# A GELU MLP on one core: the second product by 15 block products for 18

## The chip, the cores and the metric

One core of a Trainium2 chip. The time is device microseconds of the program on that core, as the median of the runs; a profiled execution gives the trace from which everything else is read. Engines: PE multiplies (PEld is its weight load), DVE is the vector engine, ACT the scalar engine, POOL and SP issue transfers (POOL also has a few small operations).

## The reference

```python
def setup_inputs():
    batch, m, k, h, n = 16, 512, 768, 3072, 768     # x, w1, b1, w2: float32, random

def reference(x, w1, b1, w2):
    y = np.matmul(x, w1) + b1
    y = 0.5 * y * (1.0 + erf(y / np.sqrt(2.0)))
    return np.matmul(y, w2).astype(np.float32)
```

The 8192 rows of x go through 768 -> 3072 -> 768. The kernel multiplies in bfloat16 and sums in float32.

## The kernel before

The 8192 rows are cut into pairs of row blocks: ten pairs of 2 x 384 rows and a last one of 2 x 256. For each pair the first product fills `g` (3072 hidden values of the pair's rows, as 24 chunks of 128 hidden values, bf16), and then the second product reads `g`. A tile is 128 rows; a pair has six tiles, the last pair four.

**First product.** Pair 0 is computed plainly (`plain`: six matmuls of 384 columns for each of the 24 hidden chunks and each half). From pair 1 on, a 2 x 2 scheme with seven products P1 to P7 is used (`product1`): three matmuls each, 21 for one step j, and one step gives two hidden chunks for both halves. The scheme needs sums of x (`sum_x`, k = 0 to 3, into `xft`; P7 reads the last of them) and seven forms of each w1 block. The forms are made once on chip (`make_w1`: one copy by ACT and five block sums on DVE, twelve times), staged in whatever tile is free, written to the DRAM tensor `w1f`, and read back from there by SP into a ring of seven slots in `w1t` (`load_slot`, asked for when a slot's last product P3 has been issued). DVE evacuates three products of a step (P7, P2, P6), ACT one (P1), and ACT does the four gelus. Pair 1 does its first three steps plainly, since their w1 blocks are still raw in `w1t`.

**Second product.** Each of the three sub-blocks of a pair takes one tile of the upper half and one of the lower half, with the hidden dimension cut in two and the output columns in two: a 2 x 2 scheme with seven products (M1 to M7), each of 12 matmuls 128 x 128 x 384 (`part2`). Five of the left operands are sums of parts of `g` (`gsum`, DVE, 1536 elements per partition, into `st`), two are parts of `g` itself. The seven forms of w2 lie in `w2t`; five of them are made from the four raw blocks by DVE (`make_w2`). Each product has one evacuation (`evacuate`): five on DVE, two on ACT. There are three PSUM pools of 3, 3 and 2 buffers.

**Order.** All work is put in program order by hand (`inorder`), so each engine works through its own list. The first two products of the next pair, P1 and P7, are issued before the current pair's last product (`ahead`), to cover the evacuations at the boundary; the sums of x for the next pair stand behind the last sub-block's M1, M5 and M2:

```python
            rest(2, "M1", forms(1) if later else xsums(0, 1))
            rest(2, "M5", forms(1) if later else xsums(2))
            rest(2, "M2", forms(1) if later else xsums(3))
            rest(2, "M7")
            if nxt is not None and p > 0:
                ahead(p + 1)
            rest(2, "M6")
```

In pair 0 the `make_w1` calls lie among the plain products (three) and among the second product (six); the last three stand at the start of pair 1, ahead of its plain products. Loads of x, w1 and w2, and the output stores of all pairs but the last, are issued from POOL; the w1f stores, the slot loads, the transposes of x and the last pair's outputs from SP.

Of the kernel before, what the change touches and what calls it, by code (L numbers as in the profile page):

```python
# [14 lines left out]

WF = {"M3": 0, "M4": 1, "M1": 2, "M5": 3, "M2": 4, "M6": 5, "M7": 6}
# [3 lines left out]
SF = {"M1": 0, "M5": 1, "M2": 2, "M7": 3, "M6": 4}  # L28
BANK = {"M1": "Z", "M3": "Y", "M2": "Y", "M6": "Y", "M4": "X", "M5": "X", "M7": "X"}
# [3 lines left out]
def kernel(  # L33
# [19 lines left out]
    HW = 384  # L53
    SLOT = 7 * KH * P
    RAW = 4 * KH * P
    RING = 7
    PLAIN = 3
    GRP = 3 * KC * P
    FIRST = -(-PLAIN * RAW // SLOT)
# [10 lines left out]
    w2r = w2.rearrange("(hh j p) n -> p j hh n", p=P, hh=2)  # L70
# [8 lines left out]
    evp = ctx.enter_context(tc.tile_pool(name="evp", bufs=2))  # L79
    x1p = ctx.enter_context(tc.tile_pool(name="x1p", bufs=1))  # L80
    xbp = ctx.enter_context(tc.tile_pool(name="xbp", bufs=2))
    dram = ctx.enter_context(tc.tile_pool(name="dram", bufs=1, space=bass.MemoryType.DRAM))
    ps_x = ctx.enter_context(tc.tile_pool(name="ps_x", bufs=3, space=bass.MemoryType.PSUM))
    ps_y = ctx.enter_context(tc.tile_pool(name="ps_y", bufs=3, space=bass.MemoryType.PSUM))
    ps_z = ctx.enter_context(tc.tile_pool(name="ps_z", bufs=2, space=bass.MemoryType.PSUM))

    w1f = dram.tile([HP, P, SLOT], BF16, name="w1f")
    w2t = keep.tile([P, HP, 7, NB], BF16, name="w2t")
    w1t = keep.tile([P, RING * SLOT], BF16, name="w1t")
    xt = keep.tile([P, KC, 2, HW], BF16, name="xt")  # L90
    xft = keep.tile([P, 5, KH, HW], BF16, name="xft")
    g = keep.tile([P, HC, 2, HW], BF16, name="g")
    st = keep.tile([P, 5, HP, P], BF16, name="st")
    tt = keep.tile([P, 2, 4, HW], FP32, name="tt")
    ot = keep.tile([P, 4, N], FP32, name="ot")
    b1t = keep.tile([P, HC], FP32, name="b1t")
    ident = keep.tile([P, P], BF16, name="ident")
# [15 lines left out]

    def bank(t, m):
        b = BANK[m]
        if b not in t:
            pool = {"X": ps_x, "Y": ps_y, "Z": ps_z}[b]
            t[b] = pool.tile([P, 512], FP32, name="ps" + b.lower())
        return t[b]

    def evacuate(t, m, n, c):
        ps = t[BANK[m]][:, :n]
        if m == "M4":
            t["x1"] = x1p.tile([P, HW], FP32, name="x1")
            copy("act", t["x1"][:, :n], ps)
        elif m == "M3":
            t["q"] = evp.tile([P, HW], FP32, name="q")
            add(t["q"][:, :n], t["x1"][:, :n], ps)
        elif m == "M1":
            t["z"] = evp.tile([P, HW], FP32, name="z")  # L130
            copy("act", t["z"][:, :n], ps)
        elif m == "M5":
            sub(c["12"], ps, t["q"][:, :n])
        elif m == "M2":
            sub(c["21"], ps, t["q"][:, :n])
        elif m == "M7":
            sub(c["11"], t["z"][:, :n], ps)
        else:
            sub(c["22"], t["z"][:, :n], ps)

# [9 lines left out]

    def moving1(m, kc, w):
        if m in XRAW:
            kh, half = XRAW[m]
            return xt[:, kh * KH + kc, half, :w]
        return xft[:, XF[m], kc, :w]

    def gelu1(j, h, half, src, w, sign):
        hc = h * HP + j  # L160
        inorder(nc.scalar.activation(out=g[:, hc, half, :w], in_=src, func=ACTF.Gelu,  # L161
                                     bias=b1t[:, hc:hc + 1], scale=sign))

    def product1(t, m, p, j, w):
        if m == "P1":
            t["c12"] = ps_z.tile([P, 512], FP32, name="psz")
            ps = t["c12"]
        elif m == "P4":
            ps = t["c12"]
        elif m == "P7":  # L170
            t["c22"] = ps_y.tile([P, 512], FP32, name="psy")
            ps = t["c22"]
        elif m == "P5":
            ps = t["c22"]
        else:
            ps = t["c11"]
# [6 lines left out]
        ps = ps[:, :w]  # L183
        if m == "P1":
            t["c11"] = ps_x.tile([P, 512], FP32, name="psx")
            copy("act", t["c11"][:, :w], ps)
        elif m == "P7":
            t["v"] = evp.tile([P, HW], FP32, name="z")
            copy("dve", t["v"][:, :w], ps)
        elif m == "P2":  # L190
            sub(t["c22"][:, :w], ps, t["v"][:, :w])
        elif m == "P6":
            sub(tt[:, j % 2, 0, :w], ps, t["v"][:, :w])
        elif m == "P4":
            gelu1(j, 1, 0, ps, w, 1.0)
        elif m == "P3":
            load_slot((p - 1) * HP + j - PLAIN + RING)
            gelu1(j, 0, 0, ps, w, 1.0)
        elif m == "P5":
            gelu1(j, 0, 1, tt[:, j % 2, 0, :w], w, -1.0)  # L200
            gelu1(j, 1, 1, ps, w, -1.0)


    def rows(h, half, i, j0=0, j1=HP):
        return g[:, h * HP + j0:h * HP + j1, half, i * P:(i + 1) * P]

    def gsum(m, i, j0=0, j1=HP):
        dst = st[:, SF[m], j0:j1, :]
        a11, a21 = rows(0, 0, i, j0, j1), rows(0, 1, i, j0, j1)
        a12, a22 = rows(1, 0, i, j0, j1), rows(1, 1, i, j0, j1)  # L210
        if m == "M1":
            add(dst, a11, a22)
        elif m == "M5":
            add(dst, a11, a12)
        elif m == "M2":
            add(dst, a21, a22)
        elif m == "M7":
            sub(dst, a22, a12)
        else:
            sub(dst, a11, a21)  # L220

    def part2(t, m, i, j0, j1):
        ps = bank(t, m)
# [381 lines left out]
```

## Time and profile before

| | |
|---|---|
| median of 3 runs | 903.23 us (902.63 to 903.81) |
| profiled execution | 901.76 us |
| its span, first to last instruction | 900.0 us |
| granted PE clock | 1.000 |
| PE busy | 890.6 us, 99% of the span |
| DVE busy | 479.8 us, 53% |
| ACT busy | 371.1 us, 41% |
| POOL busy | 81.4 us, 9% |
| second product's matmuls (L231) | 2688 |
| first product's matmuls (L179) | 2457 |

A group's line names the line of the kernel, the engine, the operation, the tiles (output <- inputs), the shapes and the count, then the busy time in total, the mean of one in ns, and the idle time of the engine just before these instructions with what ended it. Lines L101, L108 and L111 are the helpers `copy`, `add` and `sub`, so their groups are told apart by the tiles: `st<-g` is a sum for the second product, `ot<-...` an evacuation, `xft<-xt` a sum of x. A matmul's shown duration (326 ns) contains the pipeline behind it; matmuls follow each other closer than that. "DVE ot <- PE psx" at the end of a line means that the instruction started when PE's write to psx was done. POOL and SP show only the issue of a transfer; the page's last part has the median time to its landing.

### The profile page before, as it was taken

How to read it: one execution, taken by the hardware profiler on the slowest of the kernel's cores; microseconds unless marked ns; L12 is line 12 of the kernel's file. 1: busy time of each engine (PE TensorE's matmuls, PEld its weight loads, DVE VectorE, ACT ScalarE, POOL GpSimd, SP SyncE). 2: the span in 40 equal slices, each digit the busy share in tenths (PEclk: the TensorE clock that was granted, in tenths of full speed). 3: DMA queues.
4: the chain of work that ended last, by engine and by line, in shares of the span. 5: the costliest groups of instructions: out<-in, count | busy, mean ns of one | idle time of the engine just before them, and what ended most of it. 6: DMA issues, size and time to landing. Idle time of an engine off the chain costs nothing.

```text
span 900.0 us, 14009 instructions
## 1 busy us (share of the span) xinstructions
PE 890.6 (99%) x5627; PEld 544.6 (61%) x5627; DVE 479.8 (53%) x844; ACT 371.1 (41%) x726; POOL 81.4 (9%) x148
## 2 busy tenths in 40 slices
PE   7999999999999999999999999999999999999998
PEld 5656656666666666666666666665666666666774
DVE  1287744654555374456455544654564455446445
ACT  3542473057117503730671175047206702740550
POOL 5201100100110010001001100100100011000000
PEclk9999999999999999999999999999999999999999
DMA  9997976456817674673567267646636682673501
GB/s 163 207 232 180 391 268 173 109 161 202 179 62 211 203 134 112 201 174 101 174 212 158 74 208 193 141 118 211 157 94 194 204 147 86 215 176 104 163 27 71
DMA packets 89158, 148.30 MB, mean 165 GB/s; under 512 B 50796, under 2 KB 68228, under 8 KB 89092
## 3 DMA queue, kind: packets, MB, share of 16 engines
q1 hardware_dynamic: 65588, 101.77, 38.7%
q0 software_dynamic: 23504, 45.62, 22.9%
q8 instruction: 44, 0.72, 0.3%
q14 instruction: 22, 0.18, 0.1%
HBM read 124.56 MB, written 33.42 MB: 176 GB/s over the span
## 4 chain that ended last, share of the span: by engine, by line
PE 98%; DMA 1%; ACT 0%; POOL 0%; issue 0%; DVE 0%; ACTq 0%; POOLq 0%
PE psx L231 21%; PE psy L231 21%; PE psx L179 18%; PE psz L179 12%; PE psy L179 12%; PE psz L231 7%; PE psy L337 3%; PE psx L337 3%; DMA st<-in_x_dram 1%; PE psy L400 0%; ACT g L161 0%; PE psx L400 0%; PE psz L366 0%; DVE psy L111 0%; POOL st L76 0%
## 5 line engine op out<-in xcount | busy, mean ns | idle before, releaser
L179 PEld LDWEIGHTS <-w1t 128*128 128x128 bf16 x2457 | 240.2, 98 | 147.4 <-issue 0.8
L231 PEld LDWEIGHTS <-st 128*128 128x128 bf16 x1920 | 187.9, 98 | 124.0
L231 PE MATMUL psx<-w2t,st 128*128 128x384 bf16 x768 | 135.3, 326 | 0.0
L231 PE MATMUL psy<-w2t,st 128*128 128x384 bf16 x768 | 135.3, 326 | 0.0
L179 PE MATMUL psx<-xft,w1t 128*128 128x384 bf16 (+1 forms) x702 | 131.0, 320 | 0.0
L111 DVE TENSOR_TENSOR tt<-psx,z 128x384 f32<-128x384 f32 (+1 forms) x117 | 63.6, 544 | 103.0 <-PE psx L179 103.0
L101 ACT COPY x<-psx 128x384 f32<-128x384 f32 x32 | 15.3, 478 | 229.0 <-PE psx L231 228.0
L231 PEld LDWEIGHTS <-g 128*128 128x128 bf16 x768 | 75.1, 98 | 50.0 <-issue 0.6
L101 ACT COPY psx<-psz 128x384 f32<-128x384 f32 (+1 forms) x117 | 53.0, 453 | 94.4 <-PE psz L179 94.4
L108 DVE TENSOR_TENSOR st<-g 128x1536 bf16<-128x1536 bf16 (+2 forms) x116 | 91.7, 812 | 0.0
L111 DVE TENSOR_TENSOR psy<-psx,z 128x384 f32<-128x384 f32 (+1 forms) x117 | 64.7, 553 | 49.3 <-PE psx L179 47.6
L103 DVE COPY z<-psy 128x384 f32<-128x384 f32 (+1 forms) x117 | 63.7, 544 | 39.3 <-PE psy L179 39.2
L161 ACT ACTIVATE g<-psx,b1t 128x384 bf16<-128x384 f32 (+1 forms) x117 | 66.6, 569 | 38.5 <-PE psx L179 37.0
L161 ACT ACTIVATE g<-psz,b1t 128x384 bf16<-128x384 f32 (+1 forms) x117 | 66.5, 569 | 26.6 <-PE psz L179 26.6
L76 POOL DMA_DIRECT2D xb<-in_x_dram x58 | 31.2, 542 | 499.4 <-DMA xt<-xb 491.9
L161 ACT ACTIVATE g<-tt,b1t 128x384 bf16<-128x384 f32 (+1 forms) x117 | 70.9, 606 | 11.5 <-DVE tt L111 11.5
L179 PE MATMUL psx<-xt,w1t 128*128 128x384 bf16 (+1 forms) x351 | 74.2, 320 | 0.2
L179 PE MATMUL psz<-xt,w1t 128*128 128x384 bf16 (+1 forms) x351 | 74.2, 321 | 0.0
L179 PE MATMUL psy<-xt,w1t 128*128 128x384 bf16 (+1 forms) x351 | 74.2, 321 | 0.0
L179 PE MATMUL psy<-xft,w1t 128*128 128x384 bf16 (+1 forms) x351 | 74.2, 321 | 0.0
L179 PE MATMUL psz<-xft,w1t 128*128 128x384 bf16 (+1 forms) x351 | 74.2, 321 | 0.0
L231 PE MATMUL psx<-w2t,g 128*128 128x384 bf16 x384 | 74.2, 326 | 0.0
(58 smaller groups left out, 653.3 us busy)
## 6 DMA issues: line engine op xcount, KB each, us to landing
w1t<-w1f SPq DMA_DIRECT2D x117, 672.0 KB, 5.3
out_dram<-ot POOLq DMA_DIRECT2D x60, 384.0 KB, 2.6
xb<-in_x_dram POOLq DMA_DIRECT2D x58, 192.0 KB, 4.0
w2t<-in_w_dram POOLq DMA_DIRECT2D x8, 576.0 KB, 22.5
w1t<-in_w_dram POOLq DMA_DIRECT2D x7, 576.0 KB, 19.0
w1f<-tt SPq DMA_DIRECT2D x6, 672.0 KB, 5.6
w1f<-xft SPq DMA_DIRECT2D x4, 672.0 KB, 4.8
out_dram<-ot SPq DMA_DIRECT2D x4, 384.0 KB, 2.5
```

What stands on the lines that cost most here:

```text
L76: inorder(queue.dma_start(out=out, in_=in_))
L101: inorder(nc.scalar.copy(out=dst, in_=src))
L103: inorder(nc.vector.tensor_copy(out=dst, in_=src))
L108: inorder(nc.vector.tensor_tensor(out=dst, in0=a, in1=b, op=ALU.add))
L111: inorder(nc.vector.tensor_tensor(out=dst, in0=a, in1=b, op=ALU.subtract))
L161: inorder(nc.scalar.activation(out=g[:, hc, half, :w], in_=src, func=ACTF.Gelu, bias=b1t[:, hc:hc + 1], scale=sign))
L179: inorder(nc.tensor.matmul(out=ps[:, :w], lhsT=forms[:, W1F[m], kc, :], rhs=moving1(m, kc, w), start=(kc == 0 and m in ("P1", "P7")), stop ...
L231: inorder(nc.tensor.matmul(out=ps[:, :NB], lhsT=lhs, rhs=w2t[:, j, WF[m], :], start=(j == 0 and m in ("M1", "M3", "M4")), stop=(j == HP - ...
L337: inorder(nc.tensor.matmul(out=py[:, :HW], lhsT=lhs[:, kc, (j % 3) * P:(j % 3 + 1) * P], rhs=xt[:, kc, half, :], start=(kc == 0), stop=(kc ...
```

## The change

The second product goes from a 2 x 2 scheme to one with blocks of 3 x 3 x 2: a group is three row tiles; the hidden dimension is cut into three pieces of 8 chunks, the output columns into two halves. Plain blocks would take 18 block products; the scheme takes 15 (M0 to M14), each of 8 matmuls 128 x 128 x 384.

- A pair has two groups, G0 (the upper half's tiles) and G1 (the lower half's). The last pair has one group and one tile that is left over and computed plainly, but for two differences of its parts that go with raw w2 blocks.
- Six left operands are parts of `g` as they are (M14, M8, M4, M7, M6, M13). Nine are sums, made by 15 DVE instructions of 1024 elements; three of the nine (M3, M11, M0) are made in place in `g`, six in `st` (seven slots of 1024). `place_h` orders the hidden chunks in `g` so that each piece is contiguous.
- Of the 15 forms of w2 in `w2t`, four are raw blocks and eleven are made by DVE.
- Products share PSUM buffers in chains: A holds M4, then M12, M10 and M11 on top of it; B holds M13, M1, M9, M0; C M14, M2; D M8, M3; M5, M6 and M7 have one each. After each link the buffer's running sum is added to its place in the output tile. Per group: 6 copies on ACT, 12 additions on DVE.
- All PSUM buffers come from one pool of eight.
- The sums EARLY (M2a, M3a) and MIDDLE (M12, M2b, M10a, M11a, M11b) of a pair are spread over the later steps of its first product (`fill`, behind P2 and P6).
- The sums of x for the next pair now stand behind the second group's M3, M10, M9 and M11; `ahead` follows, then M0.
- To make room, the ring of w1 slots has five places for seven, and raw w1 groups 2 and 3 lie in `xft`. `make_w1` is staged in other tiles: three calls after the plain group 3, one after group 5, two in pair 0's G1, six at the start of pair 1. The first four stores to w1f go through POOL.
- w2 is loaded in eight transfers by chunk, in another order among the w1 loads.

```diff
+NF = 15
+WF = {"b11": 0, "b12": 1, "b21": 2, "b22": 3, "b31": 4, "b32": 5,
+      "M2": 0, "M3": 1, "M7": 2, "M10": 3, "M9": 4, "M0": 5, "M1": 6, "M14": 7,
+      "M11": 8, "M12": 9, "M8": 10, "M4": 11, "M5": 12, "M6": 13, "M13": 14}
+BANK = {"M4": "A", "M12": "A", "M10": "A", "M11": "A", "M13": "B", "M1": "B", "M9": "B", "M0": "B",
+        "M14": "C", "M2": "C", "M8": "D", "M3": "D", "M5": "5", "M6": "6", "M7": "7"}
+OPENS = ("M14", "M8", "M4", "M7", "M6", "M13", "M5")
+LHS = {"M14": (1, 0), "M8": (0, 0), "M4": (2, 1), "M7": (1, 1), "M6": (0, 2), "M13": (2, 2),
+       "M3": (2, 0), "M11": (0, 1), "M0": (1, 2)}
...
-    RING = 7
+    RING = 5
...
+    psp = ctx.enter_context(tc.tile_pool(name="psp", bufs=8, space=bass.MemoryType.PSUM))
...
+    def gsum(G, m):
+        a = lambda i, k: block(G, i - 1, k - 1)
+        if m == "M2a":
+            sub(form(G, "M2"), a(3, 1), a(2, 1))
+        elif m == "M2b":
+            sub(form(G, "M2"), form(G, "M2"), a(3, 2))
+        elif m == "M3a":
+            sub(a(3, 1), a(3, 1), a(1, 1))
+        elif m == "M3b":
+            sub(a(3, 1), a(3, 1), a(3, 3))
...
+        elif m == "M9a":
+            sub(form(G, "M9"), a(2, 3), a(3, 3))
+        elif m == "M9b":
+            add(form(G, "M9"), form(G, "M9"), a(2, 2))
+        elif m == "M0a":
+            sub(a(2, 3), a(1, 3), a(2, 3))
+        elif m == "M0b":
+            add(a(2, 3), a(2, 3), a(2, 1))
...
+    def finish2(G, m):
...
+        if m == "M14":
+            copy("act", c(2, 1), ps)
...
+        elif m == "M7":
+            copy("act", c(1, 1), ps)
+            add(c(2, 1), c(2, 1), ps)
+        elif m == "M6":
+            copy("act", c(2, 2), ps)
+            add(c(1, 2), c(1, 2), ps)
...
+        elif m == "M5":
+            sub(c(1, 1), c(1, 1), ps)
+            add(c(2, 2), c(2, 2), ps)
+        else:
+            o = {"M12": (3, 2), "M2": (3, 1), "M1": (3, 1), "M3": (3, 2), "M10": (1, 2), "M9": (2, 1),
+                 "M11": (1, 1), "M0": (2, 2)}[m]
+            add(c(*o), c(*o), ps)
+            if m in ("M3", "M11", "M0"):
+                send(o[0])
...
+    def make_w2(c0, c1):
+        f = w2t[:, c0:c1]
+        b = lambda n: f[:, :, WF[n], :]
+        add(b("M4"), b("b11"), b("b21"))
+        add(b("M13"), b("b12"), b("b32"))
+        sub(b("M1"), b("M13"), b("b31"))
...
+    stage = ((otf, 0), (otf, N * 4), (evf, 0), (xftf, 0), (evf, 0), (xftf, 0),
+             (stf, 0), (stf, SLOT), (otf, 0), (otf, N * 4), (stf, 0), (stf, SLOT))
...
+        queue = nc.gpsimd if made < 4 else nc.sync
...
+    load_w1(2)
+    load_w1(3)
+    load_w2(0)
+    load_w2(1)
+    for gi in range(4, 8):
         load_w1(gi)
...
+        if gi < 7:
+            load_w2(gi - 2)
+    for c in range(5, QC):
+        load_w2(c)
...
+        if gi == 3:
+            for _ in range(3):
                 make_w1()
+            make_w2(2, 4)
+            for G in blk:
+                for m in EARLY:
+                    gsum(G, m)
+        if gi == 5:
+            make_w1()
+            for m in MIDDLE:
+                gsum(blk[0], m)
+            make_w2(4, 6)
+            make_w2(6, 7)
+    make_w2(7, 8)
...
+    def middle(G, extra):
+        rest(G, "M12", gsums(G, "M5") + extra(0))
+        rest(G, "M2", gsums(G, "M9a", "M9b") + extra(1))
+        rest(G, "M1", gsums(G, "M0a", "M0b") + extra(2))
+        rest(G, "M5", extra(3))
+        rest(G, "M3", extra(4))
+        rest(G, "M10", extra(5))
+        rest(G, "M9", extra(6))
+        rest(G, "M11", extra(7))
...
             if p == 1:
-                while made < HP:
-                    make_w1()
+                form_w1()
+                form_w1()
                 for k in range(4):
                     sum_x(k, w)
+                for _ in range(4):
+                    form_w1()
                 for hc in hcs:
                     plain(hc, 0)
                     if hc == hcs[-1]:
                         ahead(p)
                     plain(hc, 1)
                 load_raw_slots(PLAIN)
...
+            def fill(s):
+                for first_j in (QH, 2 * QH):
+                    if 0 <= s <= last and js[s] > first_j and todo[first_j]:
+                        todo[first_j].pop(0)()
+                        return
...
             step1(last, "P5")
+            part2(G0, "M14", range(0, 5))
             step1(last, "P3")
+            part2(G0, "M14", range(5, QC))
+            finish2(G0, "M14")
+            left = todo[QH] + todo[2 * QH]
+            for m in ("M8", "M4", "M7"):
+                rest(G0, m)
+                for f in left[:1]:
+                    f()
+                left = left[1:]
+            qs = [h * QH + q for q in range(QH) for h in range(2)]
+            part2(G0, "M6", qs)
+            finish2(G0, "M6")
+            gsum(G0, "M1")
+            part2(G0, "M13", qs)
+            finish2(G0, "M13")
+            for m in ("M3b", "M10b"):
+                gsum(G0, m)
+            for f in left:
+                f()
+        else:
+            raws = ("M4", "M14", "M13", "M8", "M7", "M6")
+            for c in range(QC - 1):
+                for m in raws:
+                    part2(G0, m, (c,))
+            for m in raws:
+                part2(G0, m, (QC - 1,))
+                finish2(G0, m)
+            for m in ("M1", "M3b", "M10b"):
+                gsum(G0, m)
...
+        if p == 0:
+            mid = gsums(G1, *MIDDLE)
+            middle(G0, lambda n: mid[n - 3:n - 2] if 3 <= n < 8 else [])
+        else:
+            middle(G0, lambda n: [])
+        rest(G0, "M0")
+
+        if full:
+            rest(G1, "M14", gsums(G1, "M1"))
+            rest(G1, "M8", gsums(G1, "M3b"))
+            rest(G1, "M4", gsums(G1, "M10b"))
+            rest(G1, "M7", [form_w1] if p == 0 else ())
+            rest(G1, "M6")
+            rest(G1, "M13")
+
+            def extra(n):
+                if p == 0:
+                    return [form_w1] if n == 6 else []
+                return [lambda: sum_x(n - 4, nxt[1])] if 4 <= n < 8 else []
+            middle(G1, extra)
             if p > 0:
                 ahead(p + 1)
+            rest(G1, "M0")
```

`rest(G, m, after)` issues a product's eight matmuls, its evacuation (`finish2`), and then the operations in `after`; `form_w1` is `make_w1` and then whatever slot loads have become possible.

## The prediction

> **What bounds the kernel now.** I read the page first (engine totals, then the chain of work that ended last), then the busy times of one whole pair, then the vector engine's groups by shape, then the order of time where two pairs meet.
>
> From the page, totals and chain:
>
> ```profile
> PE 890.6 (99%) x5627; PEld 544.6 (61%) x5627; DVE 479.8 (53%) x844; ACT 371.1 (41%) x726; POOL 81.4 (9%) x148
> ...
> PE 98%; DMA 1%; ACT 0%; POOL 0%; issue 0%; DVE 0%; ACTq 0%; POOLq 0%
> ```
>
> Busy times of one pair (columns: stretch, length, PE, PEld, DVE, ACT, POOL, clock, DMA share, GB/s):
>
> ```profile
> 143.40:225.30 81.90, 81.90 (x506) 49.32 (x504) 44.12 (x73) 33.85 (x66) 6.48 (x12) 1.00 0.59 160
> ```
>
> A pair has 252 + 252 = 504 matmuls and takes 81.90 us: 0.1625 us each, without a gap. So every matmul saved is worth 0.1625 us, and every microsecond for which PE has to wait is lost: there is no idle time in which to hide it.
>
> DVE groups, shapes apart (line, name, count | busy us, mean ns):
>
> ```profile
> L108 DVE TENSOR_TENSOR st<-g 128x1536 bf16<-128x1536 bf16 x76 | 72.2, 950 | 0.0
> L108 DVE TENSOR_TENSOR q<-x,psy 128x384 f32<-128x384 f32 x32 | 17.6, 551 | 79.3 <-ACT x L101 64.2 <-PE psy L231 15.1
> L108 DVE TENSOR_TENSOR xft<-xt 128x1152 bf16<-128x1152 bf16 x9 | 6.8, 752 | 0.0
> L108 DVE TENSOR_TENSOR tt<-w1t 128x768 bf16<-128x768 bf16 x6 | 3.3, 552 | 0.0
> ```
>
> In order of time, where pair 1 hands over to pair 2, and one stretch of DVE before it:
>
> ```profile
> 153.00 1.82 DVE L111 TENSOR_TENSOR st<-g 128x1536 bf16<-128x1536 bf16 x2
> 154.97 0.56 DVE L111 TENSOR_TENSOR ot<-psx,q 128x384 f32<-128x384 f32 x1
> 155.45 0.95 DVE L108 TENSOR_TENSOR st<-g 128x1536 bf16<-128x1536 bf16 x1
> ...
> 181.45 0.75 DVE L108 TENSOR_TENSOR xft<-xft,xt 128x1152 bf16<-128x1152 bf16 x1
> 182.56 0.91 PEld L179 LDWEIGHTS <-w1t 128*128 128x128 bf16 x6
> 182.72 0.65 PE L179 MATMUL psz<-xft,w1t 128*128 128x384 bf16 x3
> 182.99 0.55 DVE L111 TENSOR_TENSOR ot<-z,psx 128x384 f32<-128x384 f32 x1 [0.80 <-PE psx L231]
> 183.21 0.65 PE L179 MATMUL psy<-xft,w1t 128*128 128x384 bf16 x3
> ```
>
> Two sums end 1.82 us after the first began, so the second starts 0.87 after the first (0.95 long): a queued DVE instruction starts 0.08 before the end shown of the one ahead. Likewise 0.48 (154.97 to 155.45) from an evacuation to the next. And the last sum of x (k=3) is done at 182.20, a microsecond before P7's matmuls read it at 183.21: today that is hidden.
>
> **Durations I use.** bf16 sums run 552, 752 and 950 ns at 768, 1152 and 1536 elements, a straight line: 0.685 us at 1024, and 0.60 from start to start. Evacuation 0.555, start to start 0.48. Sum of x 0.75 and 0.67. A sum that reads the result of the one just ahead costs 0.13 more (the xft sums at L275 and L277 start 0.80 to 0.84 apart). A consumer starts about 0.05 after its producer.
>
> **Matmuls removed.** Before: 2688 at L231 (768+768+384+384+384). After: 21 groups x 15 products x 8 chunks = 2520, and 6 x 8 = 48 for the one tile left over: 2568. 120 x 0.1625 = 19.50 us less, all on the path. One product now lasts 8 x 0.1625 = 1.30 us, not 1.95: DVE has less time behind each.
>
> **DVE work per pair.** Sums: 30 x 0.60 = 18.0 (before: 15 x 0.87 = 13.1). Evacuations: 24 for 15. With the first product (36 x 0.48) and the x sums, about 49 us of 80: no bound on average. What counts is where the queue is late.
>
> **First product, with up to 14 sums filled in.** A step is 21 x 0.1625 = 3.41. DVE then has 3 x 0.48 + 2 x 0.60 = 2.64. A fill after P6 makes P7's copy 0.1 late, whose reader comes 0.9 later: 0. In the last pair (step 2.38, two fills a step) 2.25 of 2.38: 0. If that cover went, 0.2 a step over 5 steps.
>
> **First group of a pair (G0).** Zero at M14. DVE: M6's add 7.03, then M1, M3b, M10b and the leftover M11b (4 x 0.60) to 9.91; M12's add and M5's sum to 10.99; M2's add; two sums for M9 (1.33); M1's add; two for M0 (1.33); M5's two adds; M3's, to 16.06. M10's add ends 16.7; M11, which needs its buffer A back, starts at 17.39. Nothing waits: 0, with 0.7 to spare.
>
> **Second group, and the hand-over: the step that costs.** The sums of x are now strung behind M3, M10, M9 and M11 (before: behind M1, M5 and M2), with `ahead` right after M11. Zero at the group's M14, a product ends every 1.30: M2 at 10.40, M11 at 18.20, P1 at 18.69. From M2 on DVE is never idle: from 10.44, 8 evacuations x 0.48 = 3.84, four sums 4 x 0.60 + 2 x 0.13 = 2.67, three x sums 2.01, and the last one 0.75: done at 19.71, P7 may start at 19.76. PE wanted it at 18.69: 1.07 us idle, and M0 and the next pair's first step stand behind P7 on PE and shift with it. Floor: M11's add cannot start before 18.24, so 18.24 + 0.48 + 0.75 + 0.05 = 19.52, 0.83 idle however quick the rest. Nine hand-overs (pairs 1 to 9): 9.65 us, at least 7.5.
>
> **Prologue and pair 0.** The same sixteen loads of 576 KB go through POOL's queue; they land 2.88 us apart (w2t issued 36.42, landing 22.5 later: 58.9). Later w1 groups fall back one or two places; the last lands at 50.4, its matmuls begin at 53.7: 0. Forming w2 is now 11 sums for each of 8 chunks: two chunks 11 x 0.47 + 0.4 = 5.6, one 11 x 0.27 + 0.4 = 3.35. DVE, in order: chunks 2-3 when chunk 3 lands, 41.9 to 47.5; EARLY, make_w1 (1.28) and MIDDLE to 54.3; chunks 4-5 to 59.9; 6 to 63.3; 7 to 66.65. PE reaches chunk 7 at 59.5 + 7 x 0.975 = 66.4 and reads the ninth form at 67.1: just no wait. But DVE is late: M1, M3b, M10b end 70.5, M12's add 71.0, M5's sum is ready at 71.7 where PE wants it at 71.25 (0.44); five sums of G1 (3.0) then stand between the adds, so M10's comes at 78.4 and M11 waits 1.54 for buffer A. Sum 1.98; 0 to 5 if the last load comes 3 us later or earlier. At the start of that product the page's PE wait of 0.34 at 60.43 (one of three psy buffers) goes, since eight are shared: -0.3.
>
> **Start of pair 1.** Six make_w1 stand here instead of three, and ACT's copies for them are ahead of the plain products' gelus. The last two are staged in st and wait for two w1f stores to land. Those are issued near 102.7 and 104 (plains start at 100.6). I take 5.6 us for a store (w1f<-tt): ACT's last copy starts 109.6, the first gelu ends 111.0; PE has filled its eight buffers at 108.4: 2.65 idle, and 0.2 at P2. With 3.2 us (the quickest store) 0.2 in all, with 10.6 (w1f<-st) 7.7. I take 2.9: between 5.6 and 10.6 I stay near 5.6 because fewer slot loads run beside them than before.
>
> **At nothing.** Ring of 5 slots, not 7: a slot is asked for 4 x 3.41 - 2.44 = 11.2 us ahead, landing takes 5.3 (last pair 7.8 against 4.0 to 5.4); uncovered, some 2 us each. M8's copy in G1 waits about 1 us for an output store; M3, the next user of its buffer, is 9 us later. The xb loads on POOL end some 16 us into the second product, as M3's output store is due: 0. The left-over tile has 16 matmuls (2.6 us) before its first sum is read: 0.
>
> **Sum.** 901.76 (the profiled execution) - 19.50 + 9.65 + 1.98 + 2.9 - 0.3 = 896.5. The median of the runs lies 1.47 above the profiled one: **898.0**.
>
> **Rivals.**
> *The whole gain stays*: the x sums are hidden as today. 901.76 - 19.5 = 882.3, with the offset 883.7. For it: PE never waits now. Against: the 0.83 floor, which holds whatever DVE did before. 0.10.
> *Slower, in-place sums*: nine of fifteen sums write over one of their operands, and no row shows that. Each dearer by d adds 3d at a hand-over, 6d - 0.72 in G0 (ten times, once d is over 0.12) and 5d in pair 0. The gain is gone at 16.9 us of such stalls (19.5 + 0.3 - 2.9), which is d = 0.14. At 0.2 they are 22.8: 907.7, with the offset 909. The far end, one element at a time as fp32 rows run (555 ns at 384, so 1.22 at 1024), d = 0.54: 58 us, 944. The other end is 0, like every bf16 row here, and I take that one. 0.18.
> *Slower, whole durations*: DVE instructions follow without overlap (0.685, 0.555, 0.75). Hand-over 2.09, G0 0.40, pair 0 3.2: 9 x 2.49 + 0.4 + 3.2 = 26.0; 910.9, with the offset 912. Against it stand 1.82 us for two sums of 0.95. 0.02. [...]
> *Moderate extra stalls* (sums at 0.65 to 0.70, stores at 10 us, a late load), which eat 4 to 8 of the gain: 902 to 905. 0.10.
>
> **How the numbers follow.** Forecast 0.60, the rest as above. A change under 0.2% (1.8 us) is about what a measurement here cannot tell from none: 901.4 to 905.0. Faster: 0.60 + 0.10 and a little of the moderate case, 0.71; same: 0.09; slower: the two slow rivals, 0.20. The forecast's own range is 892 to 901 (store 3.2 and no wait in pair 0, to store 7 and sums at 0.65). For 8 in 10 it reaches 889 to 907, into the whole gain (0.09 below) and the in-place case (0.11 above).
>
> **What would show it.** Right: 2568 matmuls at the second product's line; PE waiting about 1.1 us, nine times, on the DVE sum into xft before P7; M11 in pair 0 held by an add into ot; gelus late after copies to st near 109. Wrong: no wait on xft; st or g sums of 128x1024 longer than 0.70 us; PE waits within G0 of every pair; a wait on w1t.

## The result, and the profile after

The changed kernel takes 903.93 us (median of 20 runs, 902.47 to 907.67) against 903.00 for the kernel before, measured beside it (20 runs, 899.91 to 904.14). The ratio is 1.0019, 95% interval 1.0010 to 1.0028: 0.9 us slower between the medians, 1.7 us by the ratio; nothing is left of the time that the matmuls save. The forecast was 898.0, in a range of 892 to 901, and "faster". The kernel before was also measured beside each series of experiments below, at 902.9 to 903.0, so that their times can be compared. The profiled execution took 905.50 us, span 903.7, where the profiled one of before took 901.76, span 900.0.

On the page of the changed kernel, the engine totals, the chain of work that ended last, and two rows of the groups (line, engine, tiles, count | busy, mean ns | idle before, what ended it). L147 is the first product's matmul, L221 the second product's, L382 the plain product's; L102 is `copy`, L109 `add`, L112 `sub`, L136 the gelu, L79 a transfer:

```profile
PE 878.2 (97%) x5507; PEld 536.0 (59%) x5507; DVE 574.7 (64%) x1068; ACT 397.6 (44%) x790; POOL 83.7 (9%) x152
...
PE 85%; DVE 10%; DMA 3%; issue 1%; ACT 1%; POOL 0%; DVEq 0%; ACTq 0%; SPq 0%; POOLq 0%
...
L221 PE MATMUL ps<-w2t,g 128*128 128x384 bf16 x1512 | 257.5, 326 | 1.3 <-DVE ot L109 1.3
...
L221 PE MATMUL ps<-w2t,st 128*128 128x384 bf16 x1008 | 171.0, 326 | 1.4 <-DVE st L109 0.8
```

5627 - 5507 = 120 matmuls are gone, as the change says (1512 + 1008, and 48 of the left-over tile at L631). PE's share of the last chain went from 98% to 85%: the engine that never waited now does. For what it waits, in the waits of PE (what PE's instruction wrote, for which engine and tile; us in total, times, longest):

```profile
PE ps L147 <- DVE xft L109: 8.3, 9, 0.9
PE ps L382 <- ACT g L136: 6.1, 1, 6.1
PE ps L445 <- DMA w1t<-in_w_dram: 3.1, 1, 3.1
PE ps L221 <- DVE ot L109: 1.3, 1, 1.3
...
PE ps L221 <- DVE st L109: 0.8, 1, 0.8
PE ps L147 <- DVE ps L112: 0.5, 1, 0.5
PE ps L221 <- DVE st L112: 0.3, 1, 0.3
PE ps L221 <- ACT ot L102: 0.2, 1, 0.2
```

The L445 wait, for the first piece of w1, is in both kernels. Four places are new: nine hand-overs (first line), the start of pair 1 (second), G0 of pair 0 (the waits on ot of DVE and on st), and one late fill in the last pair (ps). A small fifth one is a single wait for a copy by ACT (last line). The granted clock fell too, 0.992 on average for 1.000. By stretches of 2 us at the start of pair 1 (length, PE, PEld, DVE, ACT, POOL busy, then clock, DMA share, GB/s):

```profile
112.00:114.00 2.00, 0.00 (x0) 0.00 (x0) 2.00 (x8) 1.90 (x3) 0.00 (x0) 1.00 1.07 334
114.00:116.00 2.00, 0.00 (x0) 0.00 (x0) 1.59 (x6) 0.24 (x1) 0.00 (x0) 0.62 1.09 333
116.00:118.00 2.00, 0.53 (x2) 0.26 (x2) 1.36 (x4) 1.89 (x4) 0.00 (x0) 0.50 1.02 417
118.00:120.00 2.00, 2.00 (x8) 0.93 (x7) 0.00 (x0) 2.00 (x5) 0.00 (x0) 0.50 1.02 390
120.00:122.00 2.00, 2.00 (x10) 1.07 (x9) 0.00 (x0) 1.69 (x4) 0.00 (x0) 0.67 1.02 422
122.00:124.00 2.00, 2.00 (x14) 1.22 (x13) 0.55 (x1) 1.08 (x3) 0.00 (x0) 1.00 1.00 417
```

**The account**, span of 900.0 to span of 903.7. Matmuls -19.50. Nine hand-overs, gap from start to start, +9.75. Start of pair 1 +8.14: 6.27 idle, and then 18 matmuls in 4.80 us where 18 at 0.1625 take 2.93. Pair 0 +2.91 (0.50, 0.97 and 1.44 ahead of M1, M5 and M11). Last pair +0.63. The one wait for ACT's copy, in G1 of pair 2, +0.39 from start to start. A psy buffer wait that is gone, -0.34. Up to the first plain product +1.89: there this execution had a granted clock of 0.50 from 10 to 15 us, the profiled one of before 1.00. Together +3.9, where +3.7 was measured.

### The profile page after: what moved, and what is told of

Read it like the earlier page. It is cut to its first block, busy times and chain, and to the rows that moved or that the text cites. A ratio compares the mean times of both kernels' runs of the same rounds, so it can differ in the third digit from the quotient of the medians.

```text
span 903.7 us, 14021 instructions
## 1 busy us (share of the span) xinstructions
PE 878.2 (97%) x5507; PEld 536.0 (59%) x5507; DVE 574.7 (64%) x1068; ACT 397.6 (44%) x790; POOL 83.7 (9%) x152
## 4 chain that ended last, share of the span: by engine, by line
PE 85%; DVE 10%; DMA 3%; issue 1%; ACT 1%; POOL 0%; DVEq 0%; ACTq 0%; SPq 0%; POOLq 0%
PE ps L147 41%; PE ps L221 36%; PE ps L382 5%; DVE ot L109 4%; DVE xft L109 1%; DVE st L112 1%; DMA w1f<-st 1%; DVE st L109 1%; PE ps L445 1%; DMA w1t<-in_w_dram 1%; PE ps L631 1%; DVE xft L112 1%; DVE g L112 1%; DVE g L109 1%; DMA out_dram<-ot 1%
## 5 line engine op out<-in xcount | busy, mean ns | idle before, releaser
L147 PEld LDWEIGHTS <-w1t 128*128 128x128 bf16 x2457 | 240.2, 98 | 158.1 <-issue 12.2
L147 PE MATMUL ps<-xft,w1t 128*128 128x384 bf16 (+1 forms) x1404 | 263.4, 320 | 8.3 <-DVE xft L109 8.3
L136 ACT ACTIVATE g<-ps,b1t 128x384 bf16<-128x384 f32 (+1 forms) x411 | 222.3, 570 | 88.0 <-PE ps L147 67.3
L221 PE MATMUL ps<-w2t,g 128*128 128x384 bf16 x1512 | 257.5, 326 | 1.3 <-DVE ot L109 1.3
L109 DVE TENSOR_TENSOR ot<-ot,ps 128x384 f32<-128x384 f32 x231 | 123.9, 550 | 136.8 <-ACT ot L102 100.1
L221 PEld LDWEIGHTS <-g 128*128 128x128 bf16 x1512 | 147.9, 98 | 98.9 <-issue 1.5
L147 PE MATMUL ps<-xt,w1t 128*128 128x384 bf16 (+1 forms) x1053 | 205.0, 320 | 0.7 <-DVE ps L112 0.5
L221 PE MATMUL ps<-w2t,st 128*128 128x384 bf16 x1008 | 171.0, 326 | 1.4 <-DVE st L109 0.8
L102 ACT COPY ot<-ps 128x384 f32<-128x384 f32 x128 | 58.0, 485 | 238.2 <-PE ps L221 181.7
L221 PEld LDWEIGHTS <-st 128*128 128x128 bf16 x1008 | 98.4, 98 | 67.4 <-DVE st L109 1.2
L102 ACT COPY ps<-ps 128x384 f32<-128x384 f32 (+1 forms) x117 | 52.9, 452 | 134.6 <-PE ps L147 134.4
L112 DVE TENSOR_TENSOR ev<-ps,ev 128x384 f32<-128x384 f32 (+1 forms) x117 | 63.6, 544 | 72.7 <-PE ps L147 72.0
L112 DVE TENSOR_TENSOR ps<-ps,ev 128x384 f32<-128x384 f32 (+1 forms) x117 | 64.7, 553 | 44.9 <-PE ps L147 42.9
L79 POOL DMA_DIRECT2D xb<-in_x_dram x58 | 31.2, 542 | 487.2 <-DMA xt<-xb 485.1
L136 ACT ACTIVATE g<-ev,b1t 128x384 bf16<-128x384 f32 (+1 forms) x117 | 70.9, 606 | 11.6 <-DVE ev L112 11.5
L112 DVE TENSOR_TENSOR st<-g 128x1024 bf16<-128x1024 bf16 x107 | 72.9, 682 | 0.0
L112 DVE TENSOR_TENSOR g<-g 128x1024 bf16<-128x1024 bf16 x84 | 57.4, 683 | 0.1
L79 POOL DMA_DIRECT2D out_dram<-ot x60 | 32.6, 543 | 242.7 <-DVE ot L109 237.2
L382 PE MATMUL ps<-xt,w1t 128*128 128x384 bf16 x252 | 43.6, 335 | 6.1 <-ACT g L136 6.1
L382 PEld LDWEIGHTS <-w1t 128*128 128x128 bf16 x252 | 25.3, 100 | 23.7 <-issue 8.4
L109 DVE TENSOR_TENSOR st<-st,g 128x1024 bf16<-128x1024 bf16 x42 | 28.9, 688 | 0.7
```

Of the source, the lines that this page charges most:

```text
L79: inorder(queue.dma_start(out=out, in_=in_))
L102: inorder(nc.scalar.copy(out=dst, in_=src))
L109: inorder(nc.vector.tensor_tensor(out=dst, in0=a, in1=b, op=ALU.add))
L112: inorder(nc.vector.tensor_tensor(out=dst, in0=a, in1=b, op=ALU.subtract))
L136: inorder(nc.scalar.activation(out=g[:, place_h(hc), half, :w], in_=src, func=ACTF.Gelu, bias=b1t[:, hc:hc + 1], scale=sign))
L147: inorder(nc.tensor.matmul(out=ps[:, :w], lhsT=forms[:, W1F[m], kc, :], rhs=moving1(m, kc, w), start=(kc == 0 and m in ("P1", "P7")), stop ...
```

## Why the hand-over waits

The theory: the chain at the end of G1 (M10's, M9's, M11's additions and the sums of x between them, in DVE's queue) ends behind PE. In order of time, DVE and then PE:

```profile
190.85 0.54 DVE L109 TENSOR_TENSOR ot<-ot,ps 128x384 f32<-128x384 f32 x1
191.31 0.75 DVE L112 TENSOR_TENSOR xft<-xt,xft 128x1152 bf16<-128x1152 bf16 x1
191.98 0.54 DVE L109 TENSOR_TENSOR ot<-ot,ps 128x384 f32<-128x384 f32 x1
192.45 0.75 DVE L109 TENSOR_TENSOR xft<-xft,xt 128x1152 bf16<-128x1152 bf16 x1
```

```profile
191.66 0.65 PE L147 MATMUL ps<-xft,w1t 128*128 128x384 bf16 x3
193.25 0.65 PE L147 MATMUL ps<-xft,w1t 128*128 128x384 bf16 x3 [0.94 <-DVE xft L109]
```

P1 starts at 191.66, M11's addition at 191.98, the last sum of x behind it at 192.45, and P7 when that has ended. If it is only the place in the queue, moving the sums up must take the wait away. **e1_xsums_early** puts them behind G1's M7, M6 and M13:

```diff
-            rest(G1, "M7", [form_w1] if p == 0 else ())
-            rest(G1, "M6")
-            rest(G1, "M13")
+            rest(G1, "M7", [form_w1] if p == 0 else xs[0:1])
+            rest(G1, "M6", xs[1:2])
+            rest(G1, "M13", xs[2:4])
```

> Edit: in pairs 1 to 9 the four sums of x stand behind the second group's M7, M6 and M13 (one, one, two) instead of behind M3, M10, M9 and M11; nothing else. Theory A (the hand-over wait is the place of these sums in DVE's queue): in the profile of the changed kernel P7 starts 1.10 us late at eight hand-overs and 0.95 at the ninth, 9.75 us in all. Behind M7 to M13 DVE has 3 x 1.30 us of product time for 2 evacuations (0.96) and 4 sums (about 2.8), so nothing becomes late: no wait on xft is left, pair period 79.95 us, time 903.9 - 9.75 = 894.2, ratio to before 0.990. Rival B (the wait only moves): DVE then evacuates M13 to M2 late and M12 or M5 waits on an addition into ot or a sum in st instead; ratio stays over 0.996. Rival C (the x rows have not arrived that early): the sums wait for the transposes, the wait on xft becomes longer, ratio over 1.00.

Measured: 902.34, ratio 0.9983 (0.9973 to 0.9993), where theory A had 894.2. The wait on xft is gone, and another has its place, as rival B had it:

```profile
PE ps L221 <- DVE st L109: 6.1, 7, 1.4
```

That is M5's sum. DVE in G1 of the same run:

```profile
254.77 0.69 DVE L109 TENSOR_TENSOR st<-st,g 128x1024 bf16<-128x1024 bf16 x1
260.64 0.55 DVE L109 TENSOR_TENSOR ot<-ot,ps 128x384 f32<-128x384 f32 x1 [5.18 <-ACT ot L102]
261.11 0.75 DVE L112 TENSOR_TENSOR xft<-xt 128x1152 bf16<-128x1152 bf16 x1
```

For 5.18 us DVE has nothing that it may do: M7's addition waits for a copy by ACT. ACT's copy of M8 stands ahead of that one and itself waits ("259.37 ... [4.49 <-DMA out_dram<-ot]") for an output store. With four output tiles used in turn, G1's M8 takes the tile that G0 has sent last, behind M0, and only one product, M14, lies between. The sums of x then come after those 5 us, in the way of M5's sum.

**e1_xsums_one_up** moves each sum of x by one product only, behind M5, M3, M10 and M9 (`sum_x(n - 3, ...)` for `3 <= n < 7`).

> Edit: the four sums of x move up by one product only, behind M5, M3, M10 and M9. Theory A with the queue worked through: sum 3 ends near 18.5 us after the group's start, P7 is wanted at 18.69, so the wait on xft goes; but M10's addition now stands behind two sums of x and ends at 17.4, where M11 wants its buffer A at 16.9: a new wait of 0.5 us on an addition into ot in each of nine pairs. Net 9 x (1.08 - 0.5) = 5.2 us, 898.7, ratio 0.9955. If the queue does not carry the wait over to the shared buffer (rival: buffers in a chain cost nothing), the whole 9.75 comes: ratio 0.990.

Measured: 900.62, ratio 0.9980 (0.9967 to 0.9993); expected 898.7. The waits are as worked out: the last sum is now ahead of M11's addition, but M10's addition is later, and M11 waits for its buffer A (the wait on ot goes from 1.3 us in one to 5.0 in nine). The median is 3.3 us under the changed kernel, for 5.2 expected. The end of G1 has no room; the start has, if the copies there come in time. **e3_tiles_by_landing** takes the tiles again in the order in which they were sent:

```diff
-        nout += 1
-        return ot[:, nout % 4, :]
+        return free.pop(0)
...
             store(ot[:, G["o"][i], :], G["rows"][i - 1], G["last"])
+            free.append(G["o"][i])
```

> Edit, alone: an output tile is taken again in the order in which the tiles were sent, so that the second group's M8 takes the tile of the first group's third row block (sent after M3) and not the one sent last, after M0. Theory A (the reuse of the out tile is what makes the second group's copies late, and this lateness is only cover lost, not yet the wait that ends last): ScalarE's copy of M8 no longer waits 4 to 6 us for the output store, the few waits of TensorE on ScalarE's ot are gone, but the wait for the last sum of x before P7 stays at 0.9 x 9. Total 902.5 to 903.5, against about 903.9 of the changed kernel. Theory B (the late copies also delay the sums of x, through VectorE's queue): the wait before P7 shrinks as well, to under 0.4 each, total 897 to 899.

Measured: 903.56, ratio 1.0016 (1.0006 to 1.0026); the nine waits on xft are still there with 0.9. As theory A says, the late copy was lost cover and not yet a loss. **e3_tiles_and_xsums** joins the two edits.

> Edit: the out tiles in the order of sending, and the four sums of x behind the second group's M7, M6 and M13 as in e1_xsums_early. Theory A (there M5's sum was late only because VectorE's add for M7 waited for ScalarE's copies, and these for the output store): no wait on xft and none on M5's sum, the hand-over's 9.75 us gone but for some 0.5; total 893.5 to 895, ratio to the kernel before 0.990. Theory B (VectorE simply has too much work at the start of the second group): the wait for M5's sum stays near 0.9 x 7, total 899.5 to 902.

Measured: 894.89, ratio 0.9910 (0.9896 to 0.9924), 9.0 us under the changed kernel: nearly the whole 9.75 of the hand-over. No wait on xft is left, and none for M5's sum outside pair 0. ACT in the same G1 now copies as soon as a product is done, 1.30 apart:

```profile
255.13 0.48 ACT L102 COPY ot<-ps 128x384 f32<-128x384 f32 x1 [0.82 <-PE ps L221]
256.43 0.48 ACT L102 COPY ot<-ps 128x384 f32<-128x384 f32 x1 [0.82 <-PE ps L221]
```

Either edit alone gave 1.6 and 0.4 us, both 9.0. This is shown, then: the late sums made the wait, and the order of the output tiles kept the sums from being moved.

## Why pair 1 starts late

In order of time, ACT, in the changed kernel:

```profile
111.73 1.56 ACT L102 COPY ot<-w1t 128x768 bf16<-128x768 bf16 x2 [9.90 <-DMA out_dram<-ot]
113.40 0.83 ACT L102 COPY st<-w1t 128x768 bf16<-128x768 bf16 x1
116.11 0.83 ACT L102 COPY st<-w1t 128x768 bf16<-128x768 bf16 x1 [1.87 <-DMA w1f<-st]
116.85 3.40 ACT L136 ACTIVATE g<-ps,b1t 128x384 bf16<-128x384 f32 x7
```

The gelus (last line) stand behind copies for the forms of w1, which wait for an output store and for a w1f store. The wait for the w1f store is the one that ends last. The chain of work that ended last, in order of time (start, length):

```profile
106.85 9.18 DMA w1f<-st
116.11 0.83 ACT st L102
116.94 0.49 ACT g L136
117.47 4.96 PE ps L382 x18
```

First question: is it their place in ACT's queue? **e2_forms_late** makes two forms, the sums of x, and the other forms behind the fourth (two), the eighth and the eleventh plain product; P1 and P7 stand one plain product earlier.

> Edit: at the start of pair 1 two calls of make_w1 stay ahead of the twelve plain products; two come behind the fourth plain product, one behind the eighth, one behind the eleventh; P1 and P7 of the first step move one plain product up. All the work stays. Theory A (the loss there is the order on ACT: copies that wait for transfers to land stand ahead of the gelus which free PE's eight buffers): in the profile of the changed kernel PE idles 6.27 us there and then runs 18 matmuls in 4.80 us for 2.93, 1.87 us, at a granted clock of 0.50 to 0.67; 8.14 us in all. With the gelus ahead PE idles 0 to 1.5 us and the clock stays 1.00: 6.5 to 8 us less, 896.5, ratio 0.992 to 0.994. Rival B (the work itself is too much: six makes on ACT and DVE in a stretch of 12 us): the wait stays above 4 us, at P2 or at P6 instead, ratio over 0.998.

Measured: 901.36, ratio 0.9974 (0.9963 to 0.9984); expected 896.5. The gelus are on time, and P1 of the second step waits for its slot of w1 instead, "120.07 1.14 PE L147 ... [2.42 <-DMA w1t<-w1f]"; the clock falls to 0.50 again. The load of this slot was issued only at 112.74, behind a w1f store from ot at 112.32 (in the changed kernel the copies to ot wait for an output store, up to 111.73). Of the 8.14 us, 6.7 are still lost: 3.96 idle, and 30 matmuls in 7.63 us for 4.88. Second question: what is that clock worth by itself? **e5_dummy_matmuls** puts 44 useless matmuls behind the seventh plain product.

> Edit: the order is that of the changed kernel, but PE gets 44 matmuls of 384 columns without any use (into a buffer taken ahead of the plain products, so that seven are left for these) behind the seventh plain product: 44 x 0.1625 = 7.15 us, about the time that PE idles there (6.27 us plus the one product that finds no buffer, 0.98). This tells apart the idle time from what follows it. Theory A (the slow matmuls after the wait come from the wait): the granted clock stays 1.00 through 110 to 125 us, the 1.87 us of slow matmuls go, time 903.9 - 1.9 = 902.0, ratio 1.000 or just under. Rival B (the low clock at 115 to 122 us has another cause, the transfers at about 400 GB/s or the time since the start): clock again 0.5 to 0.67 there, ratio 1.002 or more.

Measured: 905.03, ratio 1.0019 (1.0007 to 1.0031); expected 902.0. The mechanism is as expected, clock 1.00 all through 110 to 125 us, with the DMA engines as full as in the changed kernel (share 1.01 to 1.08); from the first plain product to the first P1 it is 17.88 us for 18.87:

```profile
115.00:120.00 5.00, 5.00 (x33) 3.00 (x32) 1.55 (x5) 4.71 (x10) 0.00 (x0) 1.00 1.01 389
```

Here, then, the low clock goes with the idle time and not with the transfers: 0.50 to 0.67 behind 6.27 us idle, 1.00 with the useless matmuls in that time. Of the 1.87 us that it costs, 0.98 are spent again, because the useless matmuls hold a buffer and one plain product fewer runs ahead of the wait. The total isn't lower, its median is 1.1 us higher: in the profiled execution two waits of PE on ACT's copies, 1.4 us together, stand in later pairs. Before one of them ACT waits for an output store (6.39 us to its landing), as in e1_xsums_early; the rest of the difference is not explained.

**e2_forms_restaged** makes three forms (6, 7, 8) ahead of the plain products, staged elsewhere, to load two slots early, and the others behind the sixth and the eleventh.

> Edit: at the start of the second pair three of the forms (6, 7, 8) are made ahead of the plain products, staged in other buffers, so that two slots are loaded early; forms 9 to 11 stand behind the sixth and the eleventh plain product. Theory A (the 8.14 us of this start are one chain: the gelus stand behind form copies that wait for landings, and the clock's drop follows from the idle time): no idle time over 1 us, granted clock 1.00 between 110 and 125 us, total 6.5 to 8 us under the changed kernel, so 896 to 897.5. Theory B (the slots' loads end last, whatever the order of the forms): the wait moves to the first P1 and P7 as in e2_forms_late, clock again 0.5 to 0.7, total 900 to 901.5.

Measured: 901.49, ratio 0.9987 (0.9979 to 0.9996); expected 896 to 897.5. Theory B was nearer: PE again waits 3.3 us for a slot, though its load was issued at 105.97, and took 11.70 us in the chain; 4.7 of the 8.14 us are still lost. Two orders of the same work, and the wait moved and became smaller, but did not go. What is common to them is that the DMA engines are full, with a share of 0.99 to 1.03 from 102 to 126 us. Busy times over longer stretches (the DMA share is the last column but one), first the kernel before, then the changed one:

```profile
86.00:102.00 16.00, 16.00 (x100) 9.63 (x99) 13.78 (x31) 4.14 (x6) 1.62 (x3) 1.00 1.00 375
102.00:118.00 16.00, 16.00 (x101) 9.63 (x99) 9.31 (x21) 9.72 (x19) 1.64 (x3) 1.00 1.04 389
118.00:126.00 8.00, 8.00 (x51) 4.83 (x50) 3.66 (x7) 6.04 (x12) 0.00 (x0) 1.00 0.72 232
```

```profile
86.00:102.00 16.00, 16.00 (x101) 9.65 (x99) 10.46 (x22) 5.42 (x9) 0.54 (x1) 1.00 0.23 93
102.00:118.00 16.00, 9.89 (x60) 5.77 (x59) 12.61 (x33) 4.29 (x7) 2.17 (x4) 0.89 0.93 314
118.00:126.00 8.00, 8.00 (x40) 4.39 (x39) 1.12 (x2) 5.96 (x13) 0.00 (x0) 0.79 1.02 411
```

Before, 86 to 102 us moved 375 GB/s; after, 93. SP's queue says what: of the stores of forms that SP issues from 84 us on, eight in either kernel, the kernel before issues

```profile
86.05 2.93 SPq L76 DMA_DIRECT2D w1f<-tt  x2
...
95.14 2.48 SPq L76 DMA_DIRECT2D w1f<-xft  x2
99.25 0.32 SPq L76 DMA_DIRECT2D w1f<-tt  x1
```

five ahead of 102 us, the changed one only one:

```profile
91.72 0.35 SPq L79 DMA_DIRECT2D w1f<-ev  x1
102.91 0.32 SPq L79 DMA_DIRECT2D w1f<-xft  x1
```

The change has no `tt`, and makes six forms at the start of pair 1 where three stood. Their stores then run beside the slots' loads, and land late: the four from st after 9.2 us in the median, the two from ot after 6.4, where the one issued at 91.72 took 3.1. If that is the cause, forms must be made *earlier*, not later. **e6_forms_earlier**:

```diff
-             (stf, 0), (stf, SLOT), (otf, 0), (otf, N * 4), (stf, 0), (stf, SLOT))
+             (evf, 0), (xftf, 0), (stf, 0), (otf, N * 4), (stf, SLOT), (otf, 0))
...
-            rest(G1, "M13")
+            rest(G1, "M13", [form_w1] if p == 0 else ())
...
-                    return [form_w1] if n == 6 else []
+                    return {5: [form_w1], 6: [form_w1]}.get(n, [])
```

and in pair 1 two forms ahead of the sums of x, one behind the second and one behind the fourth plain product.

> Edit, alone on the changed kernel: forms 4 to 7 are made in the first pair's second group (behind M7, M13, M10 and M9, two of them more than before, staged in ev and xft in turn), forms 8 and 9 ahead of the sums of x, 10 and 11 behind the second and fourth plain product. Theory A (the start of the second pair is bound by transfers: in the changed kernel the DMA engines are busy for 0.07 to 0.37 of their time from 86 to 102 us and fully from 106 to 126, where the kernel before fills 82 to 118): the idle time of 6.3 us and the low clock behind it go, total 6.5 to 8 us under the changed kernel's 903.9, so 896 to 897.5. Theory B (the order of the forms on ScalarE makes the stall, not the transfers, which stay full whatever is moved): as in e2_forms_restaged a wait of 3 us stays, total 900 to 902.

Measured: 896.24, ratio 0.9931 (0.9919 to 0.9944): 7.7 us under the changed kernel, as theory A has it. The stretches of this run:

```profile
86.00:102.00 16.00, 16.00 (x100) 9.60 (x99) 12.85 (x30) 6.42 (x11) 0.54 (x1) 1.00 0.49 184
102.00:118.00 16.00, 16.00 (x101) 9.66 (x99) 11.05 (x28) 9.76 (x19) 2.16 (x4) 1.00 1.02 346
```

PE is busy throughout, at clock 1.00; two more stores have gone into the quiet stretch (DMA share 0.23 to 0.49), and the full stretch behind it, 1.02 still, makes PE wait 0.3 us (at 123.75, for a slot). The three runs together show that the order on ACT alone does not make this loss: with the gelus on time most of it stays, and with two stores moved into the quiet stretch it goes. As e6_forms_earlier also has fewer copies ahead of the gelus, no run moves the transfers alone.

## Pair 0, and the parts together

In pair 0 ACT makes the six copies of the first products one after the other. M7's is the fifth, M7's addition waits for it, and DVE has nothing to do in the meantime:

```profile
68.67 2.39 ACT L102 COPY ot<-ps 128x384 f32<-128x384 f32 x6 [6.41 <-PE ps L221]
70.72 1.02 DVE L109 TENSOR_TENSOR ot<-ot,ps 128x384 f32<-128x384 f32 x2 [4.82 <-ACT ot L102]
71.65 0.68 DVE L112 TENSOR_TENSOR st<-g 128x1024 bf16<-128x1024 bf16 x1
72.25 0.68 DVE L112 TENSOR_TENSOR g<-g 128x1024 bf16<-128x1024 bf16 x1
```

while the sums of M1, M3 and M10 (from 71.65 on) wait behind it, though their operands are long there. **e4_sums_ahead_pair0** puts these three ahead of the last chunk's products, and G1's five MIDDLE sums behind its own M14, M8, M4, M7 and M6.

> Edit: in the first pair the sums M1, M3b and M10b stand ahead of the adds of the last chunk, and the second group's five middle sums stand behind its M14, M8, M4, M7 and M6 and not in the first group's middle. Theory A (the three waits of the first pair, 0.50, 0.97 and 1.44 us, come from sums queued behind VectorE's add for M7, which waits for six copies of ScalarE): all three gone, total 2.5 to 2.9 us under the changed kernel's 903.9, so 901.0 to 901.4. Theory B (the copies end late anyhow, and M12's or M11's bank waits for them): one wait of 1 to 1.5 us stays, total 902.4 to 902.9.

Measured: 903.24, ratio 1.0003 (0.9994 to 1.0012); expected 901.0 to 901.4. The three waits did go, as theory A said, and one that neither theory had came: 3.32 us of PE at G1's M12, whose buffer a copy by ACT has to leave first. This copy waits for an output store (9.05 us to its landing), and the clock after it is 0.68 from 90 to 95 us. It is the tile sent last once more; pair 0 takes its tiles in another order, and here it is M4's. **e6_with_tiles_xsums** leaves pair 0 as it is and joins the two repairs.

> Edit: e3_tiles_and_xsums (894.9) and e6_forms_earlier together. Theory A (the hand-over's wait and the second pair's start are separate stalls that add): 886.5 to 888.5, ratio to the kernel before 0.983. Theory B (they share cover on VectorE, and moving both brings a wait back): 890 to 893.

Measured: 885.68, ratio 0.9810 (0.9796 to 0.9823): 18.2 us under the changed kernel, where the two repairs alone gave 9.0 and 7.7. They add, with 1.5 over, which is within the spread of the five runs (884.50 to 888.37). **e7_all_moved** adds e4's edit to it.

> Edit: the former, and the sums of the first pair moved as in e4_sums_ahead_pair0 (with M11's two sums behind M5 and M3). Theory A (in e4 the three waits went, and what came instead was M8's copy waiting for the output store, which the tiles in order of sending take away): 2.5 to 2.9 us under e6_with_tiles_xsums, so 884 to 886. Theory B (the first group's products then wait for ScalarE's copies of the last chunk instead): under 1 us of gain.

Measured: 885.96, ratio 0.9811 (0.9798 to 0.9824). No gain, where 2.5 to 2.9 us were expected; the reason given for e4 was only half of it. G0 runs without a wait up to 89 us, but DVE, which has G1's five sums and the four forms to do there, is full (busy 4.93, 5.00 and 5.00 us of each 5 from 90 to 105 us), and G1 waits in its place, 0.31, 1.27 and 0.28 us:

```profile
98.72 1.46 PE L221 MATMUL ps<-w2t,g 128*128 128x384 bf16 x8 [1.27 <-DVE ot L109]
```

**e7_all_moved_warm** raises `busy(5)` to `busy(19)` at the start.

> Edit: the former, and 14 more useless matmuls ahead of the first product, which cover TensorE's wait of about 3.1 us for the first piece of w1. Theory A (the granted clock of 0.50 from 10 to 15 us in most runs follows from that idle time): clock 1.00 from 10 us on, total 1.5 to 2 us lower in the median, and the spread of the runs narrower. Theory B (the clock there is not set by the idle time, or the useless matmuls delay the first product): no gain, or up to 1 us slower.

Measured: 885.58, ratio 0.9801 (0.9788 to 0.9815). The clock is 1.00 from 5 to 20 us and the wait for w1 is covered, but the median is only 0.4 lower, within the spread of four runs. The two traces show where most of the gain at the start went: the first whole plain products start 0.67 us earlier (18.78 for 19.45), but in G1 of pair 0, where DVE is full, PE then waits 0.85 us for M5's sum in place of 0.31, and pair 1 starts only 0.13 us earlier (101.62 for 101.75). What the start's clock is worth in a kernel without that wait stays open.

## Why the prediction was wrong, by its steps

- **Matmuls removed**, 19.50: right, 120 of them.
- **Hand-over**, 1.07 each, 9.65: right in place, cause and size (9.75; its removal gave 9.0). What ended the wait was the last sum of x, as said.
- **Start of pair 1**, 2.9 in a range of 0.2 to 7.7: this is the step that failed, at 8.14. The wait was where it was put (gelus behind copies to st), but it was mis-sized. The w1f store was taken at 5.6 us to its landing and took 9.2; by the prediction's own sum the 3.6 us more are as much more idle time, 2.65 + 3.6 = 6.25, and 6.27 was measured. And 1.87 us went to the lower clock behind the idle time, which had no term. The copies to ot, for which nothing was charged either, waited for an output store, but that wait ended at 111.73 and was covered by the one for the w1f store. The reason given for the short landing, fewer slot loads beside it, left out the stores: the change had moved four of them out of the stretch ahead and into this one. The trace of before had the better row. There the landing of a w1f store went by its place and not by its tile: four of the five issued between 86 and 100 us, from tt and xft, show 5.5 to 6.4 us, and the three issued between 103 and 107 us, two from st and one from tt, 10.1 to 11.2. The prediction took 10.6 for the price of st, and used the median of tt.
- **Prologue and pair 0**, 1.98: right in kind, small in size (2.91). M7's addition waits for ACT's copies, and only M5 and M11 had been seen as late; M1 is too. The last load was not late.
- **At nothing**: the fills of the last pair cost 0.63; the five-place ring, G0 of the other pairs and the left-over tile nothing, as said. M8's copy was put at a wait of 1 us; in the changed kernel ACT stands idle for the output store for 4.0 to 5.3 us in seven pairs, and 1.8 and 3.2 us in the other two. This cost only the one wait of 0.39, but it is the cover without which the sums of x can't be moved, and it made e1_xsums_early and e4 come out short, and e5 in part.
- **The offset** of 1.47 from profile to median: of the profiled runs, that of before lay below its median and that of after 1.6 above, most likely by the clock in the first 20 us. The times go with the mean clock of a run: of the kernel before, runs at 1.000 take 900.5 us in the median and runs at 0.998 take 902.9, and the profiled one had 1.000; of the changed kernel, 905.5 at 0.992, as the profiled one, and 903.9 at 0.994. In which stage the other runs had the lower clock is not on record.

The misses: 5.24 + 0.93 + 0.63 + 0.39 + 0.10 = 7.3. On the sum of 896.5 for the profiled execution, with the 1.89 of its start, that makes 905.7, where 905.50 was measured; the median lies 1.6 below. The rival that came nearest was the moderate one (902 to 905), given 0.10, by its stores at 10 us; its longer sums and its late load did not come.

The in-place rival is false: `g<-g` sums take 683 to 687 ns, `st<-g` 682 to 683. (Its far end, 58 us and 944, is 54 us and 940 by its own terms.)

```profile
L112 DVE TENSOR_TENSOR st<-g 128x1024 bf16<-128x1024 bf16 x107 | 72.9, 682 | 0.0
L112 DVE TENSOR_TENSOR g<-g 128x1024 bf16<-128x1024 bf16 x84 | 57.4, 683 | 0.1
```

The rival of whole durations is false too: in pair 0 two queued sums of 0.68 start at 71.65 and 72.25, 0.60 apart; a sum that reads the result of the one just ahead starts 0.71 behind it (74.99 and 75.70). *The whole gain stays*, 883.7, was not this kernel, but the same arithmetic comes near it with two of the stalls mended: 885.7.

## What to carry to other kernels

When a change takes work out of the bounding engine, list what the saved time and the removed buffers had been covering; a staging tile that disappears can move transfers, and the DMA share by stretches shows where they have gone (here it went from 1.00 to 0.23 from 86 to 102 us). A landing time is to be taken from the same place in the order, not from the row with the same name; the DMA share alone does not give it (at 1.00 the stores of before took 5.5 to 6.4 us, at 1.04 they took 10.1 to 11.2). A buffer reused in turn isn't reused in the order in which it comes free: look who waits for the store that was sent last, even where that wait costs nothing yet.

## What the runs showed of the hardware

Past the start of the program, the granted clock was low around idle time of PE in these places, and the slow matmuls behind it cost as well. With 6.27 us idle, up to 117.47 in the changed kernel, it was 0.62, 0.50, 0.50 and 0.67 in the four stretches of 2 us from 114 us on, and 1.87 us were lost; after 3.32 us (e4) it was 0.68 over 5 us. In e2_forms_late, with a gap of 2.58 us behind shorter ones, it was 0.72, then 0.50 for 4 us, and 2.75 us were lost. The length alone does not decide: at the start of the program gaps of 2.7 to 3.6 us were followed by a clock of 0.50 to 0.69 from 10 to 15 us in nine profiled executions, and gaps of 2.9 to 3.2 us by 1.00 in four, the kernel before among them.

A store of 672 KB to w1f took 9.2 us from st with the DMA engines full (share 1.01 to 1.05 from 106 to 118 us), and 3.1 from ev in a quieter stretch of the same run (0.37 from 90 to 94 us). What makes it 5.5 to 6.4 us in one full stretch of the kernel before (share 1.00) and 10.1 to 11.2 in the next (1.04) is not shown.
